# Layer 0's modulation by blocks: from split float32r passes with the activations stationary to plain float32 products with the raw weight block stationary

## The chip, the core and the metric

The kernel runs on one core of a Trainium2 chip. Five engines work side by side, each on its own queue of instructions in order: PE (TensorE, matrix products), DVE (VectorE), ACT (ScalarE), POOL (GpSimd) and SP (SyncE, which here only issues loads). They wait for each other by semaphores. The metric is device time of one execution in microseconds (us).

## The reference, cut to what matters

Two layers of a diffusion backbone run over 512 latent tokens and 256 context tokens, 1024 features wide. Each layer draws its shifts, scales and gates from two conditioning vectors, one per stream:

```python
c_act, cc_act = silu(c), silu(c_ctx)                # [1024] each
mod_l = c_act  @ w_mod[l] + b_mod[l]                # w_mod[l]: [1024, 6144]
mod_c = cc_act @ w_mod[l] + b_mod[l]
sh1, sc1, g1, sh2, sc2, g2 = split(mod_l, 6)        # likewise for the context
h = rmsnorm(x, g_norm1) * (1 + sc1) + sh1           # feeds the mixer's input product w_in
x = x + g1 * mixer(h); x = x + g2 * mlp(rmsnorm(x, g_norm2) * (1 + sc2) + sh2)
```

The outputs `sc1`, `sh1` of layer 0 stand ahead of everything else; `g1` and `sh2` are needed only later.

## The kernel before, in words

All matrix products keep about float32 accuracy with float32r passes, which hold fewer bits: each operand is split in a high and a low part, and three passes (high by high, high by low, low by high) add up. Weights come in blocks of 128 x 1024 float32 (512 KB). The class `Weights` streams them in the order of their use: SP loads a block into one of four `raw` buffers, ACT casts it to the high part `whi` (L142), DVE subtracts to get the low part `wlo` (L143). A `raw` buffer is free again when both are done. Loads run three blocks ahead of use, splits two. The loads of `x` stand in the same SP queue (`load`), in program order.

The modulation of a layer has three groups of 2048 outputs: group 0 is `sh1`, `sc1`; group 1 is `g1`, `sh2`; group 2 is `sc2`, `g2`. Groups 0 and 1 of layer 0 go "by blocks" on PE: 8 pieces (`n`) of 512 outputs, each from 4 weight blocks (`kk`), 32 blocks in all. All other groups go by rows on DVE (`mod_rows`, tile `junk`) and are not touched. `mod_block` makes one block: for each of its two halves of 128 features, the activations `ct` (128 x 4: high and low part of both vectors) are the stationary operand, and 512 columns of `whi`, then of `wlo`, stream through: four matmuls of 512 columns into rows 0 to 3 of the PSUM tile `modps` (L369). After the fourth block ACT copies the 4 x 512 result to `row`, PE turns it with four transposes into `modt` (L376), and two small DVE additions (L381, L385) leave the outputs on partitions.

Where these blocks stand: `first_tiles` makes pieces 2 and 3 (the scales `sc1`) first, each followed by scaling half of the features (`s`, then `xh` on ACT and `xl` on DVE), and runs the first two tiles of the input product (`lx0`, `lx1`, PSUM `inps`) on half of the features at a time. Blocks of pieces 0 and 1 (the shifts) stand between the products of the second half. Then come `spread` (1/rms of the tokens on all partitions), `first_bias` (PSUM `bias`: the shifts' product, added to the finished tiles) and the steps of the table `ORDER`; its steps `f1`, `f2`, `f4` each make one, two or four of the 16 blocks of group 1, between the products of the tiles `pu0`, `pu1`, `kv0`, `kv1`, `kr` and of the recurrent gates (`gps`). `nsum` sums the squares of `x` over the features with plain float32 products of 128 x 128 stationary and one moving column. A second kind, `lsum`, `qs`, `kns`, does the same later on.

Within each engine a scheduler orders the instructions when the kernel is built.

Of the kernel before, what the change touches and what calls it, by code (L numbers as in the profile page):

```python
# [9 lines left out]
F32 = mybir.dt.float32  # L10
F32R = mybir.dt.float32r
# [3 lines left out]
ALU = mybir.AluOpType  # L15
# [3 lines left out]
L = 512  # L19
# [7 lines left out]
EPS = 1e-6  # L27
# [9 lines left out]
KD = D // 128  # L37
# [26 lines left out]
# The engine of each kind of step, in either layer: s(calar), v(ector) or g(psimd).  # L64
# [12 lines left out]
def by_rows(l, g, h):  # L77
    """Half h of a modulation group: by rows of the transposed weight (vector engine), or by blocks (tensor engine)."""
    return l > 0 or (g, h) in ((2,0),(2,1))
# [32 lines left out]
class Weights:  # L112
    """Streams the weight blocks in the order of their use and keeps each as two parts whose sum is exact."""
# [7 lines left out]
    def advance(self, at):  # L121
        K, nc = self.K, self.K.nc
        while self.loaded < min(len(self.order), at + 1 + self.loads):
            name = self.order[self.loaded]
            raw = K.rawp.tile([128, 1024], F32, tag="raw", name="raw")
            K.load(raw, K.wb[BLOCK_AT[name]])
            self.raw[name] = raw
            self.loaded += 1
        while self.split < min(len(self.order), at + 1 + self.splits):
            name = self.order[self.split]  # L130
            raw = self.raw.pop(name)
            hi = K.wp.tile([128, 1024], F32R, tag="w", name="whi")
            if name[2:] == ("kr",):
                # Twice the same 64 columns: the first take the low part, so that one pass carries both parts.
                nc.scalar.copy(hi, raw)
                r3, h3 = (t.rearrange("p (k m) -> p k m", k=KD)[:, :, 0:64] for t in (raw, hi))
                nc.vector.tensor_tensor(h3, r3, h3.bitcast(F32), ALU.subtract)
                self.parts[name] = (hi,)
                self.split += 1
                continue  # L140
            lo = K.wp.tile([128, 1024], F32R, tag="w", name="wlo")
            nc.scalar.copy(hi, raw)  # L142
            nc.vector.tensor_tensor(lo, raw, hi.bitcast(F32), ALU.subtract)  # L143
            self.parts[name] = (hi, lo)
            self.split += 1
# [31 lines left out]
class Kernel:  # L177
# [41 lines left out]
    def times(self, what, out, in_, scale):  # L219
        """in_ times a value per partition."""  # L220
        e = PLACE[what][self.layer]
        if e == "s":
            return self.nc.scalar.activation(out, in_, AF.Copy, scale=scale)
        if e == "g":
            return self.nc.gpsimd.tensor_scalar(out, in_, scale, 0.0, ALU.mult, ALU.add)  # L225
        return self.nc.vector.tensor_scalar(out, in_, scale, None, ALU.mult)

    def plus(self, what, out, in_, bias):
        """in_ plus a value per partition."""
        if PLACE[what][self.layer] == "s":  # L230
            return self.nc.scalar.activation(out, in_, AF.Identity, bias=bias)
        return self.nc.vector.tensor_scalar(out, in_, bias, None, ALU.add)

    def mm3(self, lhs, rhs, segs, first, last):
        """Product of two split operands: segs lists (psum, lhs columns, rhs columns)."""
# [8 lines left out]
    def split(self, name, src, n):  # L244
        """The two float32r parts of src[:, :n]."""
# [5 lines left out]
    def rsqrt(self, v, n, r=None, sign=1.0):  # L251
        """sign / sqrt(v) on a tiny tile, refined by one Newton step."""
# [10 lines left out]
    def rsqrt_dve(self, v, n, r=None, sign=1.0):  # L263
        """1 / sqrt(v) on a tiny tile: a first guess from the bits of v, then three Newton steps."""
# [15 lines left out]
    def load(self, out, in_):  # L280
        """A load that keeps its place in the order of the loads."""
# [4 lines left out]
    def stage(self, name, tables=None):  # L286
        """From here on, functions of another table set: queued behind those of the set before."""
# [27 lines left out]
    def consts(self):  # L315
# [14 lines left out]
        self.ct = cp.tile([128, 8, 4], F32R, name="ct")  # L330
# [3 lines left out]
        nc.vector.tensor_copy(self.ct[:, :, 0:2], c3)  # L334
        nc.vector.tensor_tensor(self.ct[:, :, 2:4], c3, self.ct[:, :, 0:2].bitcast(F32), ALU.subtract)

    def decay(self, l):
        """-8 softplus(-lam) and its negative, softplus by max(u, 0) + log1p(exp(-|u|))."""
# [22 lines left out]
    def mod_block(self, l, g, n, kk):  # L361
        nc = self.nc
        hi, lo = self.w.get((l, "mod", g, n, kk))
# [3 lines left out]
        for j in range(2):  # L367
            for i, w in enumerate((hi, lo)):
                nc.tensor.matmul(ps[0:4, :], lhsT=self.ct[:, kk * 2 + j, :], rhs=w[:, j * 512:(j + 1) * 512],  # L369
                                 start=(kk == 0 and j == 0 and i == 0), stop=(kk == 3 and j == 1 and i == 1))  # L370
        if kk == 3:
            row = self.slot("row")
            self.move("mod.c", row[0:4, 0:512], ps[0:4, :])
            pt = self.psB("modt")
            for j in range(4):
                nc.tensor.transpose(pt[:, j * 4:j * 4 + 4], row[0:4, j * 128:(j + 1) * 128], self.ident[0:4, 0:4])  # L376
            p4 = pt[:, 0:16].rearrange("p (j h v) -> p h v j", j=4, h=2)
            at = l * NPRM + PRM["bm"][0] + g * 16 + n * 4
            b = self.prm[:, at:at + 4].unsqueeze(1).to_broadcast([128, 2, 4])
            t = self.tiny(8).rearrange("p (v j) -> p v j", v=2)  # L380
            nc.vector.tensor_tensor(t, p4[:, 1], b, ALU.add)  # L381
# [3 lines left out]
            nc.vector.tensor_tensor(m, p4[:, 0], t, ALU.add)  # L385

    def mod_rows(self, todo):
        """Modulation by rows of the transposed weight, for halves (layer, group, half): loads run one item ahead."""
# [37 lines left out]
    def norm_scale(self, l, which):  # L426
        """g * (1 + scale) for both streams; the shift's place."""
# [11 lines left out]
    def square(self, k, x, n, pool=False):  # L439
        """Adds the squares of one tile to the running sum."""  # L440
# [17 lines left out]
    def scaled(self, k, x, s, sh, ctx):  # L458
        """x * s as two parts, with the shift as further columns."""
# [12 lines left out]
    def token_sums(self, sq, cols, ps, at, step, nt, first, last):  # L472
        """ps[:, at + tt * step + ...] += column sums of sq with the selector cols, tokens on partitions."""
# [15 lines left out]
    def spread(self, r, nt):  # L489
        """A value per token, on all partitions: two psum tiles (tokens 0..511 and 512..767)."""  # L490
# [22 lines left out]
    def gemm_mod(self, ps, w, xs, ctx, hook=None, ks=range(KD), shift=True):  # L513
        """Product with the modulated stream; psum columns as the stream's, or from 256 on without ctx."""
# [18 lines left out]
    def scaled_out(self, ps, ctx, name="t"):  # L533
        """psum times the tokens' 1/rms; the bias of either stream is in columns L and L + 1."""
# [46 lines left out]
    def lru_gates(self, l, i, xc, xcs, w):  # L581
        """Sigmoid and tanh parts of both directions."""
# [58 lines left out]
    def pool_mix(self, l, i, ps, ctx):  # L641
        """Window means minus the input, for the streams apart; each as two parts."""
# [58 lines left out]
    def lat_sums(self, zs, nt):  # L701
        """Sums of squares of a low-rank stream, tokens on partitions."""
# [19 lines left out]
    def query_eps(self, zs, nt):  # L722
        """The guard of the queries' norm, QK EPS, over the squared 1/rms of their low-rank stream, which the
        product with w_uq leaves out: it divides out of the norm everywhere else."""
# [4 lines left out]
    def query_lat(self, l, j, z, n):  # L729
        """z times its norm weight, as two parts."""  # L730
# [21 lines left out]
    def tables(self, l):  # L752
        """Rotation table times the norm weights, of the queries and of the keys' shared part."""
# [8 lines left out]
    def key_rope(self, z, tk):  # L762
        """The rotated shared key part, twice in rows 64..127 of two tiles, and its sums of squares per token;
        z holds the products with the weight's low part in rows 0..63, with its high part in rows 64..127."""
# [19 lines left out]
    def values(self, l, pp, half, kvn, w, vt):  # L784
        """Values with tokens on partitions: per pair of heads and half of the keys, [128, 3, (He Le Lo Ho) x 64]."""
# [16 lines left out]
    def key_part(self, l, p, kvn, w, kx):  # L802
        """Keys of a pair of heads, unrotated part: into rows 0..63 of the two tiles; squares."""
# [14 lines left out]
    def key_sums(self, l, p, sq, krv, early):  # L818
        """1/rms of the pair's keys, tokens on partitions."""
# [11 lines left out]
    def key_scale(self, l, p, r):  # L831
        """1/rms of the pair's keys, a row per head on all partitions."""
# [35 lines left out]
    def query_scale(self, sq, ctx, early):  # L868
        """-1 / (rms sqrt(QK)) of the head's queries, per token."""
# [33 lines left out]
    def transposed(self, ps2, keys):  # L903
        """Two query tiles' weights with keys on partitions: per half of the keys [128, 3, 256], as two parts."""
# [40 lines left out]
    def first_tiles(self):  # L945
        """The first products start on half of the features, and before the shift is there: its product is added
        to the finished tiles."""
# [74 lines left out]
    def mixer(self, l):  # L1022
        """The steps of a mixer, in the order of ORDER."""
# [145 lines left out]
        def project(h, m, ks):  # L1169
            """Adds the products of some of the parts to a tile of the output projection."""  # L1170
# [11 lines left out]
        def add_to(h, m, src):  # L1182
            """The tile of the residual stream with the gated product added."""
# [184 lines left out]
def _tables():  # L1368
    """Constants of the shapes: rotation factors, reciprocal window counts, selectors."""
# [34 lines left out]
def _rows(w, k):  # L1404
    """[K, M] -> [128, k tiles of M]: contraction rows on partitions."""
# [101 lines left out]
```

## Time and profile before

| | |
|---|---|
| median of 3 runs | 1653.0 us (1649.77 to 1654.8) |
| span of the profiled execution | 1650.7 us |
| PE | 96% of the span, 9519 matmul records |
| DVE, ACT, POOL | 68%, 41%, 22% |
| mean granted TensorE clock | 0.978 of 2.4 GHz |

Only the span of the profiled execution is listed; its last instruction ends with it. It lies 2.3 us under the median and within the range of the three runs. "Busy" of PE counts each matmul from its start to its modelled end, and these overlap: a busy PE can be a slow PE. The granted clock is the share of 2.4 GHz that PE got (1.00, or 0.50 at 1.2 GHz).

### The profile page before, as it was taken

The numbers are of one execution on the slowest core, as the hardware profiler recorded it, in microseconds if no ns is written. First come the engines' busy times: TensorE is split into PE (matmuls) and PEld (weight loads), VectorE is DVE, ScalarE is ACT, GpSimd is POOL, SyncE is SP. The second block draws the span as 40 slices with busy tenths as digits, with TensorE's granted clock in tenths as the row PEclk, the third lists the DMA queues.
The fourth block names the chain that finished last, engine by engine and source line by source line (L and its number), as shares of the span: only waits on it lengthen the run. The fifth ranks groups of instructions, "written<-read, shape, count | busy, mean of one in ns | idle before, by whom it ended". The sixth has DMA issues, their size and how long they took to land.

```text
span 1650.7 us, 24064 instructions
## 1 busy us (share of the span) xinstructions
PE 1582.8 (96%) x9519; PEld 1380.6 (84%) x9519; DVE 1122.0 (68%) x1810; ACT 680.4 (41%) x1078; POOL 368.2 (22%) x376
## 2 busy tenths in 40 slices
PE   5989999999999999999999999888999999999998
PEld 3668888889888888888888889787888989989897
DVE  8797888998767557837737646698987654545352
ACT  5557556646433123123213333745665432323131
POOL 4175434542300000000000232356454000000000
PEclk7999989999999999999999999999999999999999
DMA  6545211354234423524523430320334323323302
GB/s 251 198 150 185 81 58 37 94 185 152 82 97 144 142 89 119 187 78 128 166 90 120 142 109 21 121 71 20 97 122 141 103 90 96 97 90 93 100 27 102
DMA packets 54016, 184.57 MB, mean 112 GB/s; under 512 B 6624, under 2 KB 7264, under 8 KB 53904
## 3 DMA queue, kind: packets, MB, share of 16 engines
q1 hardware_dynamic: 49680, 166.49, 31.0%
q0 software_dynamic: 4224, 16.55, 2.8%
q8 instruction: 75, 1.23, 0.3%
q14 instruction: 37, 0.30, 0.1%
HBM read 170.90 MB, written 12.12 MB: 111 GB/s over the span
## 4 chain that ended last, share of the span: by engine, by line
PE 76%; DVE 15%; issue 4%; ACT 3%; POOL 1%; DMA 1%; SPq 0%; DVEq 0%; ACTq 0%; POOLq 0%
PE f L241 55%; PE wo L241 5%; PE inps L241 4%; PE sc L241 3%; DVE wlo L143 3%; PE tp L914 2%; DVE p L897 1%; PE modps L369 1%; DVE junk L413 1%; PE qp L241 1%; PE pv L936 1%; PE pv L937 1%; DVE ptl L922 1%; PE gps L241 1%; PE kns L823 1%
## 5 line engine op out<-in xcount | busy, mean ns | idle before, releaser
L142 ACT CAST whi<-raw 128x1024 fp32r<-128x1024 f32 x210 | 219.6, 1048 | 657.2 <-PE f L241 550.7
L143 DVE TENSOR_TENSOR wlo<-raw,whi 128x1024 fp32r<-128x1024 f32 x210 | 276.3, 1318 | 35.3 <-ACT whi L142 32.6
L241 PE MATMUL f<-xh,whi 128*128 128x258 f32 (+2 forms) x1024 | 234.6, 310 | 1.0 <-DVE tf L539 1.0
L241 PE MATMUL f<-xl,whi 128*128 128x258 f32 (+2 forms) x1024 | 234.5, 310 | 0.0
L241 PE MATMUL f<-xh,wlo 128*128 128x258 f32 (+2 forms) x1024 | 234.1, 310 | 0.0
L241 PE MATMUL f<-hh,wlo 128*128 128x512 f32 (+1 forms) x768 | 232.2, 356 | 0.0
L241 PE MATMUL f<-hl,whi 128*128 128x512 f32 (+1 forms) x768 | 231.9, 356 | 0.0
L241 PE MATMUL f<-hh,whi 128*128 128x512 f32 (+1 forms) x768 | 231.3, 356 | 0.0
L1276 DVE SCALAR_TENSOR_TENSOR xo<-f,mod,xo 128x512 f32<-128x512 f32 x96 | 60.5, 658 | 195.6 <-PE f L241 195.6
L413 DVE SCALAR_TENSOR_TENSOR junk<-modraw,cb 128x1024 bf16<-128x1024 f32 x128 | 161.8, 1275 | 21.9 <-DMA modraw<-in_wb_dram 21.5
L241 PEld LDWEIGHTS f<-xh,whi 128*128 128x128 f32 x1024 | 157.8, 189 | 12.5 <-PE f L241 1.2
L241 PEld LDWEIGHTS f<-xl,whi 128*128 128x128 f32 x1024 | 158.2, 189 | 11.4
L241 PEld LDWEIGHTS f<-xh,wlo 128*128 128x128 f32 x1024 | 157.9, 189 | 11.3
L539 DVE TENSOR_TENSOR tf<-f,rb 128x770 f32<-128x770 f32 (+1 forms) x64 | 52.8, 826 | 159.1 <-PE f L241 150.2
L241 PEld LDWEIGHTS f<-hh,whi 128*128 128x128 f32 x768 | 126.5, 188 | 22.4
L241 PEld LDWEIGHTS f<-hh,wlo 128*128 128x128 f32 x768 | 126.3, 188 | 22.5
L241 PEld LDWEIGHTS f<-hl,whi 128*128 128x128 f32 x768 | 126.4, 188 | 22.3
L463 POOL CAST xh<-mod 128x2 fp32r<-128x2 f32 x24 | 10.6, 441 | 466.8 <-PE f L241 466.8
L225 POOL TENSOR_SCALAR p<-p,sm 128x768 f32<-128x768 f32 (+1 forms) x80 | 70.4, 880 | 117.3 <-DVE sm L899 81.1
L241 PE MATMUL inps<-xh,whi 128*128 128x512 f32 (+1 forms) x352 | 87.3, 331 | 7.3 <-ACT xh L467 5.6
L305 ACT ACTIVATE p<-p,sm 128x768 f32<-128x768 f32 (+1 forms) x80 | 68.2, 853 | 57.4 <-DVE p L897 56.8
L241 PE MATMUL inps<-xl,whi 128*128 128x512 f32 (+1 forms) x352 | 86.4, 326 | 3.1 <-DVE xl L468 3.1
(290 smaller groups left out, 2909.9 us busy)
## 6 DMA issues: line engine op xcount, KB each, us to landing
raw<-in_wb_dram SPq DMA_DIRECT2D x212, 512.0 KB, 3.6
modraw<-in_wb_dram SPq DMA_DIRECT2D x64, 512.0 KB, 3.5
kb<-kd POOLq DMA_DIRECT2D x16, 384.0 KB, 4.3
x<-in_x_dram SPq DMA_DIRECT2D x8, 384.0 KB, 7.0
xo<-in_x_dram SPq DMA_DIRECT2D x8, 384.0 KB, 3.4
xp<-xo POOLq DMA_DIRECT2D x8, 384.0 KB, 3.5
xo<-xp SPq DMA_DIRECT2D x8, 384.0 KB, 3.1
xd<-xo POOLq DMA_DIRECT2D x8, 256.0 KB, 2.4
```

The costliest lines, as they stand in the source:

```text
L142: nc.scalar.copy(hi, raw)
L143: nc.vector.tensor_tensor(lo, raw, hi.bitcast(F32), ALU.subtract)
L225: return self.nc.gpsimd.tensor_scalar(out, in_, scale, 0.0, ALU.mult, ALU.add)
L241: nc.tensor.matmul(ps, lhsT=a[:, ca], rhs=b[:, cb], start=first and i == 0, stop=last and i == 2)
L305: ins = self.nc.scalar.activation(out, in_, func, **kw)
L369: nc.tensor.matmul(ps[0:4, :], lhsT=self.ct[:, kk * 2 + j, :], rhs=w[:, j * 512:(j + 1) * 512], start=(kk == 0 and j == 0 and i == 0), sto ...
L413: nc.vector.scalar_tensor_tensor(junk, r, 1.0, c, ALU.mult, ALU.mult, accum_out=acc[l, g][:, v * 16 + i:v * 16 + i + 1])
L539: nc.vector.tensor_tensor(t[:, 0:n], ps[:, o:o + n], self.rb[:, 0:n], ALU.mult)
L823: nc.tensor.matmul(ps[:, tt:tt + 7:6], lhsT=sq[:, tt * 128:(tt + 1) * 128], rhs=self.cst[:, CST_SELK:CST_SELK + 2], start=True, stop=True)
L897: nc.vector.tensor_scalar(p[:, 0:keys], s, rq[:, qt:qt + 1], None, ALU.mult, ALU.min, accum_out=nb)
L914: nc.tensor.transpose(ps[:, j * 256 + q * 128:j * 256 + (q + 1) * 128], ps2[q][:, kt * 128:(kt + 1) * 128], self.ident)
L1276: nc.vector.scalar_tensor_tensor(x[:, a:a + e], ps[:, a:a + e], mod[:, v, 8 + m:9 + m], x[:, a:a + e], ALU.mult, ALU.add)
```

## The change

A block of layer 0's modulation is no longer split: its `raw` tile goes to PE as it is. `mod_block` makes eight plain float32 matmuls per block. In each, a 128 x 128 piece of the raw weight is stationary and two columns of the activations `cs` (one per conditioning vector) move. Pieces of 128 outputs land on partitions straight away, in 8 columns of `modps`, so the copy to `row`, the transposes and one of the two DVE additions go. The `raw` buffer of a modulation block is free only when PE has read it. `ct` and its two small DVE instructions go. Nearly all other lines of the difference are comments and docstrings that are taken out, which moves line numbers (a helper at L241 stands at L245 now, L369 at L373).

```diff
@@ class Weights, advance
             raw = self.raw.pop(name)
+            if name[1] == "mod":
+                self.parts[name] = (raw,)
+                self.split += 1
+                continue
             hi = K.wp.tile([128, 1024], F32R, tag="w", name="whi")
@@ consts
-        self.ct = cp.tile([128, 8, 4], F32R, name="ct")
+        self.cs2 = cs
...
-        nc.vector.tensor_copy(self.ct[:, :, 0:2], c3)
-        nc.vector.tensor_tensor(self.ct[:, :, 2:4], c3, self.ct[:, :, 0:2].bitcast(F32), ALU.subtract)
@@ mod_block
-        hi, lo = self.w.get((l, "mod", g, n, kk))
+        w = self.w.get((l, "mod", g, n, kk))[0]
...
-        for j in range(2):
-            for i, w in enumerate((hi, lo)):
-                nc.tensor.matmul(ps[0:4, :], lhsT=self.ct[:, kk * 2 + j, :], rhs=w[:, j * 512:(j + 1) * 512],
-                                 start=(kk == 0 and j == 0 and i == 0), stop=(kk == 3 and j == 1 and i == 1))
+        for i in range(4):
+            for j in range(2):
+                k = kk * 2 + j
+                nc.tensor.matmul(ps[:, i * 2:i * 2 + 2], lhsT=w[:, j * 512 + i * 128:j * 512 + (i + 1) * 128],
+                                 rhs=self.cs2[:, k * 2:k * 2 + 2], start=k == 0 and i == 0, stop=k == KD - 1 and i == 3, skip_group_check=True)
         if kk == 3:
-            row = self.slot("row")
-            self.move("mod.c", row[0:4, 0:512], ps[0:4, :])
-            pt = self.psB("modt")
-            for j in range(4):
-                nc.tensor.transpose(pt[:, j * 4:j * 4 + 4], row[0:4, j * 128:(j + 1) * 128], self.ident[0:4, 0:4])
...
-            nc.vector.tensor_tensor(t, p4[:, 1], b, ALU.add)
...
-            nc.vector.tensor_tensor(m, p4[:, 0], t, ALU.add)
+            nc.vector.tensor_tensor(m, ps[:, 0:8].rearrange("p (j v) -> p v j", v=2), b, ALU.add)
```

How the change moves instructions is seen at three places. The first is DVE's queue ahead of the first scales `s`. (`dk` are the 52 tiny steps of the decay constants, `mod` the outputs.) Before:

```order
L381 TENSOR_TENSOR ty<-modt,prm 128x8
L977 COPY ct<-cst 16x128
L353 TENSOR_SCALAR dk_7_586<-dk_7_586 128x4
L353 TENSOR_SCALAR dk_7_625<-dk_7_625 128x4
L385 TENSOR_TENSOR mod_0_183<-modt,ty 128x2x4
L352 TENSOR_TENSOR dk_7_586<-dk_7_586,dk_6_585 128x4
L352 TENSOR_TENSOR dk_7_625<-dk_7_625,dk_6_624 128x4
L965 SCALAR_TENSOR_TENSOR s_113<-mod_0_183,prm 128x2x4
```

and now, where `raw` and `whi` are those of the tiles `lx0` and `lx1`:

```order
L359 TENSOR_SCALAR dk_11_543<-dk_10_542 128x4
L359 TENSOR_SCALAR dk_11_582<-dk_10_581 128x4
L360 TENSOR_SCALAR dk_10_542<-dk_10_542 128x4
L360 TENSOR_SCALAR dk_10_581<-dk_10_581 128x4
L147 TENSOR_TENSOR wlo<-raw,whi 128x1024 x2
L381 TENSOR_TENSOR mod_0_171<-modps,prm 128x2x4
L961 SCALAR_TENSOR_TENSOR s_102<-mod_0_171,prm 128x2x4
L464 SCALAR_TENSOR_TENSOR xl<-x,s_102,xh 128x512
```

The scales stood in the midst of the `dk` steps; now they stand behind all of them and behind the two subtractions for `lx0` and `lx1`.

The second place is PE's queue in the second half of the first two tiles, where the shifts' blocks stand between products. Before:

```order
L369 MATMUL modps<-wlo,ct 4x512
L369 MATMUL modps<-whi,ct 4x512
L369 MATMUL modps<-wlo,ct 4x512
L369 MATMUL modps<-whi,ct 4x512
L369 MATMUL modps<-wlo,ct 4x512
L241 MATMUL inps<-xl,whi 128x256
L241 MATMUL inps<-xh,wlo 128x512
L241 MATMUL inps<-xh,wlo 128x256
```

and now, in a pattern that repeats six times:

```order
L245 MATMUL inps<-xh,whi 128x512
L245 MATMUL inps<-xh,whi 128x256
L245 MATMUL inps<-xl,whi 128x512
L245 MATMUL inps<-xl,whi 128x256
L245 MATMUL inps<-xh,wlo 128x512
L245 MATMUL inps<-xh,wlo 128x256
L373 MATMUL modps<-cs,raw 128x2 x8
```

Six products of the tile and the eight short products of a whole modulation block take turns.

The third place is PE's queue at the recurrent gates. Before:

```order
L369 MATMUL modps<-whi,ct 4x512
L369 MATMUL modps<-wlo,ct 4x512
L369 MATMUL modps<-whi,ct 4x512
L369 MATMUL modps<-wlo,ct 4x512
L369 MATMUL modps<-whi,ct 4x512
L241 MATMUL gps<-xch,whi 128x512
L241 MATMUL gps<-xch,whi 128x256
L241 MATMUL gps<-xcl,whi 128x512
```

and now:

```order
L373 MATMUL modps<-cs,raw 128x2 x16
L245 MATMUL gps<-xch,whi 128x512
L245 MATMUL gps<-xch,whi 128x256
L245 MATMUL gps<-xcl,whi 128x512
L245 MATMUL gps<-xcl,whi 128x256
L245 MATMUL gps<-xch,wlo 128x512
L245 MATMUL gps<-xch,wlo 128x256
L373 MATMUL modps<-cs,raw 128x2 x14
```

Around each six products of a gate stand now 12 to 16 short ones of one or two modulation blocks. SP's queue issues the same loads in the same order; from the start of the attention on, the order of all engines is that of before but for some exchanged neighbours in its first part.

## Rows read from the trace of the kernel before

**Rows 1.** The page: the span, and the granted clock in 40 slices.

```profile
span 1650.7 us, 24064 instructions
...
PEclk7999989999999999999999999999999999999999
```

**Rows 2.** Window: busy us (count) of PE, PEld, DVE, ACT, POOL; PEclk, DMA, GB/s.

```profile
0.00:40.00 40.00, 21.23 (x78) 12.21 (x79) 33.13 (x78) 21.22 (x29) 18.29 (x17) 0.79 0.65 247
```

**Rows 3.** Groups of instructions, 0 to 170 us: busy, mean ns, idle before.

```profile
L143 DVE TENSOR_TENSOR wlo<-raw,whi 128x1024 fp32r<-128x1024 f32 x44 | 62.5, 1433 | 13.4 <-ACT whi L142 13.4
L142 ACT CAST whi<-raw 128x1024 fp32r<-128x1024 f32 x45 | 46.4, 1041 | 19.0 <-PE modps L369 9.9 <-DMA raw<-in_wb_dram 5.4 <-PE inps L241 3.5
...
L369 PE MATMUL modps<-wlo,ct 128*4 128x512 f32 x64 | 28.8, 451 | 7.6 <-DVE wlo L143 7.6
L369 PE MATMUL modps<-whi,ct 128*4 128x512 f32 x64 | 28.7, 448 | 6.0 <-ACT whi L142 6.0
...
L376 PE MATMUL modt<-cst,row 4*128 4x4 f32 x32 | 3.6, 215 | 3.0 <-ACT row L216 3.0
```

**Rows 4.** The chain that ended last, 30 to 144 us: start, us, what.

```profile
30.33 4.51 DMA x<-in_x_dram
...
45.09 2.06 PE nsum L478 x12
47.15 4.71 PE modps L369 x11
...
57.99 2.88 PE modps L369 x12
...
66.64 0.80 PE spread L498 x6
...
69.29 1.92 PE bias L1008 x32
...
96.04 1.94 PE gps L241 x6
...
120.77 8.45 PE inps L241 x48
...
136.50 1.04 PE gps L241 x6
...
138.25 5.63 PE inps L528 x32
```

**Rows 5.** Timeline of PE at two places: start, us, what, records.

```profile
45.94 1.21 PE L478 MATMUL nsum<-ones,acc 128*128 128x1 f32 x5
47.01 0.59 PE L369 MATMUL modps<-wlo,ct 128*4 128x512 f32 x1
...
209.07 1.39 PE L478 MATMUL lsum<-ones,lsq 128*128 128x1 f32 x12
...
211.66 0.37 PE L241 MATMUL vps<-whi,lath 128*128 128x256 f32 x1
```

**Rows 6.** Windows of half a us: columns as in rows 2.

```profile
213.00:213.50 0.50, 0.50 (x5) 0.50 (x5) 0.44 (x1) 0.50 (x2) 0.50 (x1) 0.55 0.00 0
216.50:217.00 0.50, 0.19 (x1) 0.19 (x2) 0.48 (x2) 0.00 (x1) 0.50 (x2) 1.00 0.66 188
```

**Rows 7.** Timeline of ACT, POOL and DVE, 4 to 22 us.

```profile
4.87 1.04 ACT L142 CAST whi<-raw 128x1024 fp32r<-128x1024 f32 x1 [0.91 <-DMA raw<-in_wb_dram]
...
12.09 5.29 POOL L445 TENSOR_TENSOR sq<-x 128x768 f32<-128x768 f32 x3
...
16.01 1.39 DVE L349 TENSOR_TENSOR dk<-dk 128x4 f32<-128x4 f32 x1
...
19.20 0.16 DVE L352 TENSOR_TENSOR dk<-dk,dk 128x4 f32<-128x4 f32 x1
...
21.98 0.15 DVE L965 SCALAR_TENSOR_TENSOR s<-mod,prm 128x8 f32<-128x8 f32 x1
```

**Rows 8.** A window behind the modulation: columns as in rows 2.

```profile
172.00:176.00 4.00, 2.68 (x5) 1.51 (x5) 4.00 (x6) 0.57 (x2) 1.26 (x1) 0.51 0.46 131
```

More of the change, by code (lines that the diff above doesn't have):

```diff
@@ L366, in mod_block @@
         ps = self.modps
-        for j in range(2):
-            for i, w in enumerate((hi, lo)):
-                nc.tensor.matmul(ps[0:4, :], lhsT=self.ct[:, kk * 2 + j, :], rhs=w[:, j * 512:(j + 1) * 512],
-                                 start=(kk == 0 and j == 0 and i == 0), stop=(kk == 3 and j == 1 and i == 1))
-        if kk == 3:
-            row = self.slot("row")
-            self.move("mod.c", row[0:4, 0:512], ps[0:4, :])
-            pt = self.psB("modt")
-            for j in range(4):
-                nc.tensor.transpose(pt[:, j * 4:j * 4 + 4], row[0:4, j * 128:(j + 1) * 128], self.ident[0:4, 0:4])
-            p4 = pt[:, 0:16].rearrange("p (j h v) -> p h v j", j=4, h=2)
+        for i in range(4):
[3 more added lines that the diff above has]
+                                 rhs=self.cs2[:, k * 2:k * 2 + 2], start=k == 0 and i == 0, stop=k == KD - 1 and i == 3, skip_group_check=True)
+        if kk == 3:
             at = l * NPRM + PRM["bm"][0] + g * 16 + n * 4
             b = self.prm[:, at:at + 4].unsqueeze(1).to_broadcast([128, 2, 4])
-            t = self.tiny(8).rearrange("p (v j) -> p v j", v=2)
-            nc.vector.tensor_tensor(t, p4[:, 1], b, ALU.add)
             if (l, g) not in self.mod:
```

## The prediction

> **What bounds the kernel now.** I read the page first: the span and the slices of the clock [rows 1]. From the third slice to the last PE runs at nine tenths of full clock or more; only the start is slow. The change lies wholly within the first 150 us, and a window over the first 40 comes next [rows 2]: PE is busy 21.2 us of them and DVE 33.1, so the start waits for splits, loads and scales. The chain shows a second regime behind it [rows 4]: from `nsum` at 45.1 us to the product of `kr` at 138.25 most of it is PE, one group on the next. What lengthens PE's queue there moves the end; what relieves DVE counts only where PE waits for it. PE waited for parts of modulation blocks 7.6 + 6.0 us, and for `row` 3.0 [rows 3].
>
> **What goes.** 32 casts on ACT at 1.04 us (33 us) and 32 subtractions on DVE at 1.43 us as measured there (46 us) [rows 3]. Both are off PE, so they are worth at most PE's 13.6 + 3.0 us of waits. On PE 128 passes of 512 columns go: 0.24 us each at full clock (12 in 2.88 us) and 0.43 at half (11 in 4.71) [rows 4], together 30.7 or 54.8 us; and 32 transposes with 3.6 us busy, which overlap, so some 3 us [rows 3].
>
> **What comes.** 32 x 8 = 256 plain float32 products with a 128 x 128 stationary and two moving columns. Rows show the same shape with one column: `lsum`, `qs`, `nsum`. The 12 products of `lsum` and `qs` are 24 records (a plain float32 product is two, each with its own weight load) and take 211.66 - 209.07 = 2.59 us, so 0.108 us a record [rows 5]; at half clock five records take 47.01 - 45.94 = 1.07 us, 0.214 a record. A product costs 0.216 or 0.428 us, a block 1.73 or 3.42 us, against 0.96 or 1.71 before. All 256: 55.3 us at full clock, 109.6 at half. At full clock throughout PE gains 55.3 - 30.7 - 3 = 21.6 us of work; 16.6 us of waits go against it.
>
> **The clock is the larger term.** At 209.07 us, at full clock, PE began those 24 plain records. It had no idle time, and at 213.0 to 213.5 the granted clock fell to half (1.2 GHz), 4.0 us after they began, when products that stream 256 columns had already run for 1.4 us; it was back at 1.00 in the window from 216.5, some 4.8 us after streaming resumed [rows 5, 6].  So plain products of one or two columns do not hold the clock, though they fill PE's time. I take from these rows: it falls 4 us into a stretch ruled by such products, and rises 5 us into one ruled by streaming. Streaming products slow by 0.43/0.24 = 1.78 at half clock, plain ones by 1.98. In the new order six products of a tile (1.05 us at full) alternate with eight plain ones (1.73 us), so plain work rules [rows 4].
>
> A rule of the Trainium skill speaks otherwise (TensorE: Matmul & The Clock Gate, Part 1): the default state is throttled, activity releases it, and a PE that is kept busy without gaps stays warm. By it the sum would be that of the first rival; the row at 213 us disagrees, since PE had no gap there.
>
> **The walk along PE's queue**, by landmarks of the chain [rows 4].
>
> First scales. The blocks of piece 2 start when the first raw block has landed, at 4.87 us (where ACT began its cast before) [rows 7], at half clock: 32 x 0.428 = 13.7, so `modps` ends at 19.0 and the first block of piece 3 at 22.5. But `s` stands behind 52 `dk` steps and two subtractions on DVE. While POOL squares (three in 5.29 us from 12.09), a `dk` step of DVE waits for the POOL instruction under way: 1.39 us at 16.01, against 0.16 at 19.20, when POOL stands [rows 7]. In the new order POOL has four squares and three sums there in one go; at 1.6 us each (an estimate from the 5.29 us) they last from 10.5 to some 22 us and let through about one step each. The last 32 or so steps, which overlap to some 0.1 us apiece, take 3 us more. With the two subtractions I get 28.5 us for `s`, against 22.0; if POOL lets more through, 22. The first `xh` follows at about 29.3.
>
> First half of the tiles: 48 products of a tile are 8.45 us at full, 15.0 at half. Six plain ones stand among the first (2.6). With the rise 5 us into the streaming: 29.3 + 2.6 + 5 + 5.6 = 42.5 us.
>
> Then 26 plain products (4 us at full, 7.5 left at half: 7.2 us): `nsum` starts at 49.7, against 45.1. The loads of `x` that `nsum` needs stand in SP's queue behind one that waits for the buffer of `lx1`, so for its subtraction. They began at 30.3 before, 14.8 us ahead of `nsum` [rows 4]; now near 29, so the sums are there by 44. `nsum` at half: 2.6, to 52.3.
>
> Second half: 48 products and 56 plain ones in turn, at half clock throughout: 15.0 + 24.0 = 39.0, to 91.3; `spread` started at 66.6 before. `spread` 1.4, 16 plain 6.9: `bias` at 99.5, against 69.3: **30 us late**.
>
> `bias` 1.9, `pu0` 8.45, eight plain 1.7, `pu1` 8.45, with 2.2 us for the late rise: 22.8, so the gates start at 122.3, against 96.0. (Four of these 30 us come back: before, PE waited there for the convolution on DVE and for a split. That DVE work is done in time now.)
>
> Gates, first part: 24 products 4.2 and 54 plain 11.7 are 15.9 at full; 4 us at full and 11.9 x 1.9 at half: 26.6, to 148.9. `kv0`, pool, eleven plain, `kv1`: 8.45 + 2.2 + 1.0 + 2.4 + 8.45 = 22.5, to 171.4. Second part: 39 plain 8.4 and 24 products 4.2 are 12.6; 4 and 8.6 x 1.9: 20.3, to 191.7. `kr` started at 138.25: **53 us late**; its own rise adds 2.2.
>
> Behind it nothing changes but the phase. From 172 to 176 us PE stood 1.3 us and had half clock nearly throughout [rows 8]; DVE, which it waited for, has a head start now, so I give back 3 us. Sum: 1650.7 + 53.4 + 2.2 - 3 = 1703 us of span. The median stands 2.3 us above the span of before: **1705 us**.
>
> Edits at nothing: the `ct` steps and one small addition per piece on DVE, behind which nothing waits for long; the `raw` buffers that PE now frees. SP issues in order, so a held buffer delays the loads queued behind it, but at the 247 GB/s of the first window [rows 2] a block of 512 KB comes in 2.1 us, and PE works 3 to 5 us per block with the products between; where that cover fails a block costs 1 to 2 us, three or four times at most (5 us, in the range).
>
> **Rivals.** *The clock stays full* (0.07). PE has no idle time in the new stretches, but the row at 213 us is against it. Then: 29.3, first half to 41.3, plain and `nsum` 48.2, second half 68.7, `bias` 73, gates near 95, `kr` at 144 against 138.25: +6, about 1659 us.
>
> *Half the stretches stay full* (0.13): either the second half of the first tiles (39 shrinks to 20.5, with `spread` and its 16 products 22 us less) or both gate stretches (10.7 + 7.7 = 18 us less). For it: the rows hold only one long run of plain products at full clock, and none in which they alternate with streaming ones. Then 1683 to 1687 us.
>
> *Faster* (0.04). Relief of DVE reaches the path: `s` comes at 19.5, as soon as `modps` ends, not at 28.5. That is 9 us on the path, and 3 more of waits at the convolution; it decides only if the clock stays full from there, since the stretches cost 6 us then and 50 else. Price: 1659 - 12 = 1647 us. Against it stands the order of DVE, with the scales behind all `dk`.
>
> *No change* (0.02): the late stretches wait for something that I put on PE, and 50 us vanish in idle time that the rows do not show.
>
> **How the numbers follow.** The walk has 0.74. Its own range: `s` at 22 instead of 28.5 (-6), rises 2 us sooner at four places (-5), DVE's head start worth 8 instead of 3 (-5), against loads (+5), falls after 2 us instead of 4 (three times, +2 each) and nothing given back (+3): 1689 to 1719, widened upward for stretches whose waits I put at nothing: 1724. With the half-full case below it the range is 1678 to 1724; outside it are the rival of the full clock, faster, no change, and a tail of 0.06. Within 0.3% (5 us; less can't be told from no change with this measurement) lie no change and the edge of the full clock: 0.03. Faster 0.04, slower 0.93.
>
> **What would show it.** The windows of the changed kernel at 0.50 granted clock from the plain products ahead of `nsum` to `bias`, with PE busy all the time; `bias` near 100 us; half clock again at both gate stretches; `modps` records 0.21 us apart there; `kr` near 190 us. If `modps` records are 0.11 us apart and the clock is 1.00 in these stretches, the clock step is wrong and the result is near 1660. If `s` comes well ahead of 28 us, the step on DVE is wrong. It would also be wrong if a two-column product were costlier than a one-column one, or if PE waits for raw blocks.

## The result and the profile after

The changed kernel takes 1700.4 us (median of 4 runs, 1693.9 to 1709.4) against 1651.4 for the kernel before, measured beside it (4 runs, 1649.4 to 1654.8). The ratio is 1.0294, with a 95% interval of 1.0259 to 1.0330: 49 us slower, where 1705 (1678 to 1724) was forecast, 52 above the 1653.0 that the forecast started from. The profiled execution is the slowest of the four, so the time lost is read below from places in the program, and not from its span. One run of all those below, the fourth of `e11`, took 1.9% longer than the fastest of its kernel, and medians and ratios leave it out.

The page of the changed kernel, to be read against [rows 1]:

```profile
span 1707.6 us, 24623 instructions
...
PE 1652.9 (97%) x9871; PEld 1476.1 (86%) x9871; DVE 1079.4 (63%) x1768; ACT 646.3 (38%) x1038; POOL 355.2 (21%) x376
...
PEclk9577799899999999999999999998999999999999
```

The second slice of the clock, 43 to 85 us, fell from 9 to 5. (The first slice, 9 against 7, is no gain: the profile lists 1.00 there, but 16 records of `modps` take 3.54 us from 5.07 on, 0.221 us each, near the 0.214 of half clock in [rows 5].) Three windows show where (columns as in rows 2):

```profile
40.00:70.00 30.00, 30.00 (x164) 28.49 (x162) 6.36 (x16) 4.57 (x10) 0.00 (x0) 0.66 0.40 123
70.00:100.00 30.00, 30.00 (x147) 28.94 (x148) 6.06 (x10) 4.36 (x6) 2.21 (x21) 0.50 0.45 161
100.00:140.00 40.00, 40.00 (x225) 36.84 (x224) 21.50 (x27) 13.33 (x18) 14.03 (x18) 0.80 0.32 103
```

PE has work in every one of these 100 us, and DVE and ACT, which were to be relieved, stand nearly idle (DVE 12.4 of 60 us). Yet PE's granted clock is 0.66, then 0.50, half speed for 30 us on end. The chain of the changed kernel passes through the same stages as [rows 4] and is nothing but PE from 28.92 us on:

```profile
5.07 3.54 PE modps L373 x16
...
41.81 6.64 PE modps L373 x52
48.45 2.56 PE nsum L474 x12
...
60.61 2.13 PE inps L245 x6
62.74 3.21 PE modps L373 x16
...
87.28 1.38 PE spread L494 x6
88.66 6.62 PE modps L373 x32
95.28 3.43 PE bias L1004 x32
...
108.70 1.68 PE modps L373 x16
110.38 8.54 PE inps L245 x48
118.93 1.06 PE gps L245 x6
...
132.16 4.91 PE modps L373 x24
...
158.24 10.11 PE inps L245 x48
...
188.43 7.93 PE inps L524 x32
```

Sixteen records of `modps` (one block) take 3.21 us at 62.74 and 1.68 at 108.70; six products of a tile take 2.13 at 60.61, against 1.06 in [rows 4] (48 in 8.45). In the gates 24 records take 4.91 us, 0.205 each. Half-us windows show the granted clock change between such stretches:

```profile
46.00:46.50 0.50, 0.50 (x6) 0.50 (x5) 0.14 (x1) 0.33 (x1) 0.00 (x0) 0.86 0.85 279
46.50:47.00 0.50, 0.50 (x4) 0.50 (x4) 0.07 (x1) 0.50 (x2) 0.00 (x0) 0.50 0.97 352
...
59.50:60.00 0.50, 0.50 (x6) 0.50 (x7) 0.00 (x0) 0.00 (x0) 0.00 (x0) 1.00 0.89 369
60.00:60.50 0.50, 0.50 (x5) 0.50 (x4) 0.00 (x0) 0.00 (x0) 0.00 (x0) 0.51 0.96 393
...
100.50:101.00 0.50, 0.50 (x4) 0.41 (x3) 0.00 (x0) 0.00 (x0) 0.00 (x0) 0.53 0.45 180
101.00:101.50 0.50, 0.50 (x5) 0.46 (x4) 0.00 (x0) 0.00 (x0) 0.00 (x0) 1.00 0.06 25
```

It fell at 46.4, in the run of 52 plain records that began at 41.81, was back from 56.6 to 60.0, fell again in products that took turns with plain ones, and came back only at 101.0, in the run of `inps` products behind `bias`. PE was busy throughout. A rule of the Trainium skill (TensorE: Matmul & The Clock Gate, Part 1) says that a PE kept busy without gaps stays at full clock. These rows disagree, with busy as the profile counts it: PE at 30.00 of 30.00 us and a clock of 0.50.

### The profile page after: what moved, and what is told of

Read it like the earlier page. It is cut to its first block, busy times and chain, and to the rows that moved or that the text cites. A ratio compares the mean times of both kernels' runs of the same rounds, so it can differ in the third digit from the quotient of the medians.

```text
span 1707.6 us, 24623 instructions
## 1 busy us (share of the span) xinstructions
PE 1652.9 (97%) x9871; PEld 1476.1 (86%) x9871; DVE 1079.4 (63%) x1768; ACT 646.3 (38%) x1038; POOL 355.2 (21%) x376
## 4 chain that ended last, share of the span: by engine, by line
PE 81%; DVE 12%; issue 3%; ACT 2%; POOL 1%; DMA 1%; SPq 0%; DVEq 0%; POOLq 0%; ACTq 0%
PE f L245 53%; PE inps L245 7%; PE wo L245 5%; PE modps L373 4%; PE sc L245 3%; PE tp L910 2%; DVE wlo L147 1%; DVE p L893 1%; PE gps L245 1%; PE qp L245 1%; PE pv L932 1%; PE pv L933 1%; DVE junk L409 1%; DVE keh L221 1%; DVE rn L280 1%
## 5 line engine op out<-in xcount | busy, mean ns | idle before, releaser
L146 ACT CAST whi<-raw 128x1024 fp32r<-128x1024 f32 x178 | 186.6, 1049 | 691.8 <-PE f L245 551.5
L147 DVE TENSOR_TENSOR wlo<-raw,whi 128x1024 fp32r<-128x1024 f32 x178 | 227.3, 1278 | 56.1 <-ACT whi L146 50.1
L245 PE MATMUL f<-xh,whi 128*128 128x258 f32 (+2 forms) x1024 | 235.1, 311 | 1.0 <-DVE tf L535 1.0
L245 PE MATMUL f<-xh,wlo 128*128 128x258 f32 (+2 forms) x1024 | 234.4, 310 | 0.0
L245 PE MATMUL f<-xl,whi 128*128 128x258 f32 (+2 forms) x1024 | 234.4, 310 | 0.0
L245 PE MATMUL f<-hl,whi 128*128 128x512 f32 (+1 forms) x768 | 232.3, 357 | 0.0
L245 PE MATMUL f<-hh,wlo 128*128 128x512 f32 (+1 forms) x768 | 232.1, 356 | 0.0
L245 PE MATMUL f<-hh,whi 128*128 128x512 f32 (+1 forms) x768 | 232.0, 357 | 0.0
L245 PEld LDWEIGHTS f<-xh,whi 128*128 128x128 f32 x1024 | 158.1, 189 | 12.9 <-PE f L245 1.2
L245 PEld LDWEIGHTS f<-xl,whi 128*128 128x128 f32 x1024 | 158.0, 189 | 11.1
L245 PEld LDWEIGHTS f<-xh,wlo 128*128 128x128 f32 x1024 | 157.6, 189 | 11.3
L245 PEld LDWEIGHTS f<-hl,whi 128*128 128x128 f32 x768 | 126.6, 188 | 22.5
L245 PEld LDWEIGHTS f<-hh,wlo 128*128 128x128 f32 x768 | 126.5, 188 | 22.6
L245 PEld LDWEIGHTS f<-hh,whi 128*128 128x128 f32 x768 | 126.5, 188 | 22.1
L373 PEld LDWEIGHTS modps<-cs,raw 128*128 128x128 f32 x512 | 93.8, 283 | 7.8 <-issue 5.0
L245 PE MATMUL inps<-xh,whi 128*128 128x512 f32 (+1 forms) x352 | 93.1, 346 | 7.6 <-ACT xh L463 4.8
L373 PE MATMUL modps<-cs,raw 128*128 128x2 f32 x512 | 91.8, 312 | 5.5 <-DMA raw<-in_wb_dram 5.4
```

The costliest lines, as they stand in the source:

```text
L245: nc.tensor.matmul(ps, lhsT=a[:, ca], rhs=b[:, cb], start=first and i == 0, stop=last and i == 2)
L373: nc.tensor.matmul(ps[:, i * 2:i * 2 + 2], lhsT=w[:, j * 512 + i * 128:j * 512 + (i + 1) * 128], rhs=self.cs2[:, k * 2:k * 2 + 2], start=k ...
```

## The experiments

Three theories stood against each other. *Clock*: the plain products add some PE work, but most of the loss is that PE runs at half clock wherever products with two moving columns are frequent. *Work*: the plain products just occupy PE for longer (21.6 us by the prediction's sum), and the clock is a side effect. *Loads or weight loads*: raw buffers held by PE delay the loads, or the 512 loads of a 128 x 128 stationary keep PE slow. Ratios are to the kernel before, timed beside each.

**One half of the change at a time.** `e1` has the plain form for group 0 alone, `e2` for group 1 alone; the other half keeps the split passes of before.

```diff
+def plain(g, n):
+    return g == 0
...
-            if name[1] == "mod":
+            if name[1] == "mod" and plain(*name[2:4]):
...
```

In `e2` the condition is `g == 1`.

> Only group 0 (shifts and scales, 16 blocks) goes as plain products; group 1 goes by split passes as before. Clock theory (plain products with two moving columns fill PE but do not hold the clock, and the half-clock stretches are the larger term): the half clock runs from the plain products ahead of nsum to bias as in the changed kernel, bias stands near 95 us, and the gates are back at full clock; kr at about 160 us, +22 to +26 us on before: 1673 to 1677 us. Work theory (only the longer occupation of PE by the plain records counts, the clock is incidental): half of the 21.6 us of extra work less the waits saved, at most +11: 1662 us or less. Load theory (raw buffers held by PE delay the loads): PE would show idle time ahead of modps.

> The converse: only group 1 (gates' blocks between pu0, kv0 and the recurrent gates) goes as plain products; group 0 by split passes as before. Clock theory: bias stays near 69 us, and half clock appears in both stretches of the recurrent gates, kr at 160 to 166 us, +22 to +28 us: 1673 to 1680 us. Work theory: at most +11: 1662 us or less, with the clock at 1.00 in the gates or without effect. If the two halves add up to the whole, the two effects are independent.

`e1`: 1678.7 us, ratio 1.0161 (1.0138 to 1.0184). `e2`: 1681.8 us, 1.0182 (1.0156 to 1.0208). The chain of `e1`:

```profile
87.10 1.38 PE spread L529 x6
...
91.89 2.45 PE bias L1039 x32
...
161.35 5.65 PE inps L559 x32
```

And that of `e2`:

```profile
69.11 3.43 PE bias L1039 x32
...
92.65 1.05 PE gps L249 x6
...
113.53 4.91 PE modps L408 x24
...
161.24 5.74 PE inps L559 x32
```

In `e1` `bias` comes 22.6 us late and `kr` (the last row) 23.1: all is lost ahead of `bias`, and the gates cost what they did. In `e2` `bias` is on time to 0.2 us and `kr` 23.0 us late. `e2`'s gates run 24 plain records in 4.91 us, 0.205 each: half clock. The work theory gave either of them at most 11 us; both times lie just under 2 us above the ranges of the clock theory. PE was busy for all of 40 to 100 us in `e1`, so its loads cost nothing there. The halves by time, 25.9 and 29.0 us, add up to 54.9 against 49.0 for the whole, which the intervals, 4 to 6 us either way, do not tell apart; by `kr` they add up to 46.1 against 50.2. Where the 4 us between the halves and the whole lie was not followed.

**The same products turned round.** `e3` keeps plain float32 and raw weights, and lets 512 columns of the raw block move past the two activation columns.

```diff
-        for i in range(4):
-            for j in range(2):
...
+        for j in range(2):
+            k = kk * 2 + j
+            nc.tensor.matmul(ps[0:2, :], lhsT=self.cs2[:, k * 2:k * 2 + 2], rhs=w[:, j * 512:(j + 1) * 512],
+                             start=k == 0, stop=k == KD - 1)
...
```

> All 32 blocks stay plain float32 with raw weights and no split, but the roles are exchanged: the two activation columns are stationary and 512 columns of the raw block move; two products per block half become two per block, 64 in all, with the row copy and four transposes per piece back. Clock theory (few moving columns are at fault, not float32): the granted clock stays at 1.00 in the stretches that were at 0.50; no row shows the price of a plain product of 512 columns, by bounds 0.48 us (two records of 0.24) to 0.96 us each, 31 to 61 us of PE for 64 products: 1640 to 1682 us. If plain float32 itself cannot hold the clock: half clock in the same stretches, 1690 us or more. Load theory: raw buffers are still held by PE, so the time stays near 1700 us.

1663.3 us, ratio 1.0067 (1.0046 to 1.0087). From the chain of `e3`:

```profile
54.50 1.81 PE modps L372 x4
...
62.43 3.46 DMA raw<-in_wb_dram
```

Windows of `e3`:

```profile
40.00:70.00 30.00, 27.97 (x107) 12.11 (x106) 7.49 (x19) 7.28 (x15) 1.43 (x12) 0.97 0.50 161
70.00:100.00 30.00, 30.00 (x163) 20.25 (x162) 19.68 (x25) 12.77 (x19) 11.59 (x24) 0.97 0.34 124
100.00:140.00 40.00, 39.75 (x167) 21.81 (x165) 18.25 (x21) 10.20 (x15) 20.97 (x22) 1.00 0.53 185
```

Four records in 1.81 us are 0.905 us a product, the upper bound of what was expected, and 64 of them 57.9 us. In the changed kernel 512 records would take 53.8 us at full clock (1.68 / 16 each). So `e3` gives PE more work than the changed kernel and is 37 us faster: its clock stays at 0.97 to 1.00. It isn't float32 alone that costs the clock. But the stationary operand is another here too, so `e3` doesn't tell the few moving columns from the weight loads. The load theory has a small share at most: PE stood 2.0 us between 40 and 70 us, where the chain passes through the load of a raw block (62.43).

**As much work without the form.** `e9` is the kernel before with 96 more streaming passes.

```diff
-                nc.tensor.matmul(ps[0:4, :], lhsT=self.ct[:, kk * 2 + j, :], rhs=w[:, j * 512:(j + 1) * 512],
+                for again in range(1 + (i == 1) + (i == 1 and j == 1)):
+                    nc.tensor.matmul(ps[0:4, :], lhsT=self.ct[:, kk * 2 + j, :], rhs=w[:, j * 512:(j + 1) * 512],
...
```

> The kernel before, with three more passes of wlo by ct in each of the 32 blocks (the low part's product is added two or three times, so the modulation is off in its last bits): 96 more streaming passes of 0.24 us, 23.0 us of PE at full clock, as much as the plain products add to PE's work (21.6 us). Clock theory: PE's granted clock stays as before; what lies in PE's waits is hidden, so +8 to +18 us: 1661 to 1671 us. Work theory: a like amount of PE work costs a like time, so about as slow as the changed kernel, 1690 us or more.

1668.4 us, ratio 1.0083 (1.0070 to 1.0096): 14 to 15 us for 23 us of added work, as the clock theory had it. Its clock is 1.00 where the changed kernel's is 0.66 and 0.50:

```profile
40.00:70.00 30.00, 29.08 (x153) 17.61 (x152) 19.01 (x28) 14.79 (x23) 4.05 (x2) 1.00 0.47 155
70.00:100.00 30.00, 27.11 (x171) 20.68 (x169) 23.39 (x32) 17.46 (x24) 12.91 (x35) 1.00 0.31 105
```

**The same products with more moving columns.** `e12` and `e11` are the changed kernel with each activation column read 64 or 16 times over: 128 or 32 moving columns, the same 256 products, stationaries and places. `C` is 128 or 32.

```diff
-                                 rhs=self.cs2[:, k * 2:k * 2 + 2], start=k == 0 and i == 0, stop=k == KD - 1 and i == 3, skip_group_check=True)
+                wide = self.cs2[:, k * 2:k * 2 + 2].unsqueeze(2).to_broadcast([128, 2, C // 2])
+                nc.tensor.matmul(ps[:, i * C:(i + 1) * C], lhsT=w[:, j * 512 + i * 128:j * 512 + (i + 1) * 128],
+                                 rhs=wide, start=k == 0 and i == 0, stop=k == KD - 1 and i == 3, skip_group_check=True)
...
```

> The changed kernel with the same 256 plain float32 products and the same 128 x 128 pieces of raw weight stationary in the same places, but 128 moving columns in each: either vector's column is read 64 times over, and one column of each 64 results is used. Few-columns theory: what lost the clock is the moving columns, not float32 and not the weight loads; so the clock stands at 1.00 from nsum to bias and in the gates. A record costs at least the 0.107 us of two columns, and by the 0.45 us of 512 columns in the kernel with the roles exchanged some 0.11; 512 records take 55 to 60 us, and the time is 1655 to 1668 us though no product got shorter. Weight-load theory (512 loads of a 128 x 128 stationary, one per record, keep PE from full clock): half clock in the same stretches, 1690 us or more.

> The same with 32 moving columns (either column read 16 times over). Few-columns theory gives no number between two and 128 columns: if it behaves as two columns, half clock and about 1700 us; if it behaves as 128, full clock and about 1660 us; a part of the stretches at half clock would give 1670 to 1690. Records at 0.107 us apart at full clock and 0.214 at half in any case. Weight-load theory: as two columns, 1690 us or more.

`e12`: 1658.4 us, ratio 1.0032 (1.0017 to 1.0048). `e11`: 1679.8 us, 1.0161 (1.0144 to 1.0178). Windows of `e12`:

```profile
40.00:70.00 30.00, 30.00 (x244) 28.96 (x243) 6.78 (x19) 4.99 (x11) 2.49 (x9) 1.00 0.57 178
70.00:100.00 30.00, 30.00 (x222) 27.40 (x221) 24.13 (x29) 12.84 (x20) 14.49 (x30) 1.00 0.45 152
100.00:140.00 40.00, 39.95 (x286) 37.00 (x285) 14.59 (x19) 11.51 (x16) 19.27 (x21) 1.00 0.62 202
```

The same windows of `e11`:

```profile
40.00:70.00 30.00, 30.00 (x201) 28.64 (x200) 6.27 (x16) 4.57 (x10) 0.00 (x0) 0.83 0.47 144
70.00:100.00 30.00, 30.00 (x223) 27.44 (x222) 20.10 (x28) 12.17 (x18) 12.04 (x33) 1.00 0.50 168
100.00:140.00 40.00, 40.00 (x206) 37.70 (x204) 12.28 (x17) 9.12 (x12) 20.77 (x25) 0.66 0.41 133
```

This is the plainest test. No product got shorter (in the chain of `e12` 16 records take 1.79 us, against 1.68 in the changed kernel at full clock), none went, and the kernel is 42 us faster, with the clock at 1.00 in all three windows. The weight loads are the same 512, so they are not the cause. With 32 columns the clock fell ahead of `nsum`, at 45.2 us, stood at 1.00 again from 55.5 on while blocks and products of a tile took turns, and fell once more in the gates, at 103.3: a time in between. The chain of `e12` gives the price of the clock by stages:

```profile
46.38 1.24 PE nsum L478 x12
...
64.03 1.79 PE modps L376 x16
...
68.64 0.66 PE spread L498 x6
...
93.93 1.05 PE gps L245 x6
```

From the end of `nsum` to `spread` it needs 21.0 us, where the changed kernel needs 36.3 (51.01 to 87.28). `kr` begins at 143.6 in `e12`'s timeline, so the gates take 49.7 us against 69.5 (118.93 to 188.43). These two stages give 35 of the 45 us that lie between the two kernels at `kr`.

**The same work in another order.** In `e4` the seven blocks that alternate with the second half of the first tiles stand behind it.

```diff
-                self.mod_block(0, 0, i, k - 4)
+        for i in range(2):
+            for kk in range(4):
+                self.mod_block(0, 0, i, kk)
```

> As the changed kernel, but the seven shift blocks that alternate with the products of the second half of the first two tiles all stand behind these products: 48 streaming products in one run, then 56 plain ones. The work is the same. Clock theory: the clock rises some 5 us into the run of 48 and they end at full clock; spread starts 4 to 8 us earlier than the 87.28 us of the changed kernel, about 1693 us. Work theory and load theory: spread at the same time, no change from 1700 us.

1693.5 us, ratio 1.0247 (1.0225 to 1.0269). The chain of `e4`:

```profile
50.57 10.80 PE inps L245 x48
61.37 19.77 PE modps L373 x112
81.14 1.38 PE spread L494 x6
```

The 48 products together take 10.80 us, where 15.0 was my sum for half clock throughout, and `spread` starts 6.1 us earlier with the same instructions. The interval of the ratio just overlaps that of the changed kernel, so this reading rests on the landmarks more than on the time. A long run of plain records still loses the clock: in windows of 1 us it is 1.00 from 56 to 65 us and 0.50 from 66 on.

**The late scales.** `e5` puts the `dk` steps behind the first scales on DVE's queue, `e7` does the same to the kernel before.

```diff
-        nc.vector.tensor_scalar(t[0], lam, -1.0, None, ALU.mult)
+        ins = nc.vector.tensor_scalar(t[0], lam, -1.0, None, ALU.mult)
+        if self.w.order is not None:
+            self.tc.add_manual_dep(ins.ins, self.scales.name, mybir.DependencyInfo(
+                mybir.DependencyClass.NoSync, mybir.DependencyReason.DATA), reason="behind the scales")
...
```

> The changed kernel, with the dk steps of the decay constants put behind the first scales s in the order of DVE's queue. Collision theory (dk steps each wait for POOL's squares and hold up s): s at 19.5 to 21 us instead of 26.4, the first inps at 21 to 22.5 instead of 27.3, nsum and spread 5 to 7 us earlier than 48.5 and 87.3; about 1694 us. Rival (s waits for the raw load and the two subtractions ahead of it anyway): s at 25 us or later, no change.

> The kernel before with the dk steps behind the first scales s in DVE's queue, nothing else. If dk steps were on the path to the first scales there: s at 18 to 20 us instead of 22.0, and 0 to 3 us off the time (1650 to 1653). If the products of the start wait for something else (xl and the subtractions on DVE, loads): no change.

In the changed kernel's timeline of DVE two `dk` steps mostly take 1.5 to 1.9 us as long as POOL squares and sums, and 0.28 afterwards:

```profile
10.54 1.57 DVE L354 TENSOR_TENSOR dk<-dk,dk 128x4 f32<-128x4 f32 x2
...
20.11 1.86 DVE L355 TENSOR_SCALAR dk<-dk 128x4 f32<-128x4 f32 x2
21.89 0.28 DVE L354 TENSOR_TENSOR dk<-dk,dk 128x4 f32<-128x4 f32 x2
```

POOL in the same stretch:

```profile
12.10 4.30 POOL L441 TENSOR_TENSOR sq<-x 128x768 f32<-128x768 f32 x3
16.37 5.58 POOL L452 TENSOR_TENSOR acc<-acc,sq 128x768 f32<-128x768 f32 x3
```

In `e5` `s` starts at 20.05 instead of 26.4, still behind the two subtractions, `nsum` at 42.80 and `spread` at 81.60, both 5.7 us earlier, as expected. The time is 1698.8 us, ratio 1.0272 (1.0259 to 1.0286), where about 1694 us was expected: its interval lies within that of the changed kernel, so the gain is seen in the profile and not shown by the time. `e7`: `s` at 15.5 instead of 22.0, `nsum` only 0.6 us earlier (44.5), 1652.5 us, ratio 0.9985 (0.9974 to 0.9997): too little to call a change. In the kernel before, the start waits for other things than the scales.

**A better version?** `e10` takes the turned form of `e3` for the scales alone, `e13` the 128 columns for group 0, `e14` for group 0 and the first piece of group 1, all three with the `dk` steps behind. Their edits are those shown, with another condition in `plain` (`g == 0 and n >= 2`, `g == 0`, `(g, n) <= (1, 0)`).

> Only the 8 blocks of the scales (pieces 2 and 3 of group 0) go as plain float32 products, with the two activation columns stationary and 512 columns of the raw block moving; the other 24 blocks are split as before, and the dk steps stand behind the first scales. Clock theory: streaming plain products hold the clock, and the scales come where PE waits for DVE's splits, so s at 16 to 18 us instead of 22.0, nsum at 39 to 42 us instead of 45.1, and 3 to 6 us off: 1646 to 1650 us. Rival (the gain is lost again to a later wait, for the loads of x or the convolution on DVE): bias at 69 us as before, 1652 to 1654 us.

> A version put together from the runs: group 0 (16 blocks) as plain products with 128 moving columns, group 1 split as before, and the dk steps behind the first scales. By the pieces measured: nsum at 41 us (46.2 in the kernel with 128 columns, less the 5.5 us that the dk steps cost), bias at 67.5, then as before 26.8 us to the gates and 48.7 to lsum, which starts at 143 us against 144.8: about 1651 us, no change that can be told from before. Rival (the loads of x, queued behind the raw buffers, hold nsum back to 44 us or later): bias at 70 us, 1653 to 1655 us.

> As the version with group 0 in 128 columns, with the first piece of group 1 (4 blocks, those between pu0, pu1 and the first gate) in that form too. With all blocks plain and 128 columns the way from bias to the gates took 21.1 us against 26.8, since DVE's convolution had no subtractions in its queue, and the gates' own stretch took 7.6 us more. If the first can be had without the second: gates at 89 us against 96.0, lsum at 138 against 144.8, about 1646 us. Rival (the subtractions for the second piece stand among the convolution anyway): no gain on the version with group 0 alone, about 1651.

`e10`: 1655.8 us, ratio 1.0007 (0.9996 to 1.0018); `s` at 15.6 us, but `nsum` at 46.2 and `bias` at 70.6: the early scales gained nothing, as the rival had it, though the time lies above the rival's range too. What holds `nsum` there was not tested. `e13`: 1651.1 us, 0.9986 (0.9972 to 1.0000), `nsum` at 42.4 and `lsum` at 142.2, nearly as expected. `e14`: 1649.7 us, 0.9988 (0.9976 to 1.0001), the first gate at 90.1 where 89 was expected, `lsum` at 144.3 where 138 was. None differs from before by more than a measurement can tell. The expectation of `e14` rested on a misreading of mine, which is told in the next section.

## Why the prediction was right, point by point

The likeliest case came true, by its own mechanism. The landmarks of the walk against the chain of the changed kernel:

| start of | predicted, us | measured, us | before, us |
|---|---|---|---|
| `s` | 28.5 | 26.4 | 22.0 |
| `nsum` | 49.7 | 48.45 | 45.09 |
| `spread` | 91.3 | 87.28 | 66.64 |
| `bias` | 99.5 | 95.28 | 69.29 |
| gates | 122.3 | 118.93 | see below |
| `kr` | 191.7 | 188.43 | 138.25 |

- **Price of a record**: 0.105 us at full clock and 0.201 at half, where `lsum` and `nsum` gave 0.108 and 0.214. A second moving column cost nothing that shows.
- **Scales**: the `dk` steps ahead of `s` were the cause (`e5`), slowed while POOL worked. `s` was over-priced by 2.1 us: POOL worked from 10.6 to 21.9 us, as summed, but two steps went through with each of its seven instructions, where about one was assumed. The parts of the sum were loose besides: 5.29 us for three squares are 1.76 apiece, not 1.6, and 22 + 3 us with two subtractions of 1.43 make 27.9, not 28.5.
- **Second half at half clock**: nearly. The clock stood at 1.00 from 56.6 to 60.0 us, in the first products of that stage; 39 us were summed, 36.3 measured. With the scales it is what put `kr` 3.3 us ahead of the forecast.
- **Gates at half clock**: 69.4 us summed, 69.5 measured, and 49.7 with 128 columns. That the sum fits to 0.1 us is luck: the first part took 25.2 us for 26.6, the second 20.1 for 20.3, and between them `kv0` to `kv1` took 24.2 for 22.5, since the 22 plain records ahead of `kv1` brought half clock there too (10.11 us for its 48 products, from 158.24), which was not summed. In the second part the blocks stand 23, 8, 1 and 7 products at a time, and not 12 to 16 as in the first.
- **Raw buffers**: PE's idle time ahead of `modps` is 5.5 us in all, 5.1 of it before the first block has landed at the start, so later loads cost 0.4 us, where up to 5 were allowed for.
- **`kr` 53 us late**: 50.2. Its own rise: 2.3 us, as summed (7.93 against 5.63).
- **Given back, 3 us**: the first product of the MLP (`f`) starts at 492.9 us against 443.2, so 49.7 of the 52.5 us are left, close to the 49.0 between the medians. That DVE's head start gave them back is not shown. The profiled execution lost 5.9 us more by the first `f` of the second layer (1338.9 against 1283.3), where both kernels hold the same work; the other three runs were 7.7 to 15.5 us shorter, and what caused it stays open.

One step was misread, without harm to the sum. I took the gates to begin at 96.0 us before, and so found four of thirty us given back there. But 96.04 in [rows 4] is the second group of gate products, the first that the chain happens to hold. The timeline of the kernel before shows the first, and the wait between them:

```profile
89.35 0.51 PE L241 MATMUL gps<-xch,whi 128*128 128x512 f32 x2
...
94.60 0.59 PE L369 MATMUL modps<-wlo,ct 128*4 128x512 f32 x1 [3.81 <-DVE wlo L143]
```

From `bias` to the first gate the changed kernel lost another 3.4 us (23.6 against 20.2), by `bias` and the first products of `pu0` at half clock. The wait for `wlo` that it saves lies inside the gates' stage, which cost 48.9 us before. The sum walks forward to `kr` and has no term with the 96.0, so the error didn't reach it; in `e14`, whose gain was reckoned from it, it did.

Two readings of the kernel before were too smooth. In [rows 1] the clock is not at nine tenths from the third slice on: the sixth, from 206 us, is an 8. And of the 93 us of its chain from `nsum` to `kr`, 38 are not PE: between 80.2 and 119.7 us it runs mostly through DVE. PE itself stood 5.3 us between 89 and 120 us, so not all that lengthened its queue there had to move the end.

The rival of the full clock was priced at 1659 us, with `kr` at 144, and nothing changed but the clock. `e12`, which has that clock, takes 1658.4, with `kr` at 143.6.

## What to carry to other kernels

A product with few moving columns can be dear beyond its own time: where plain float32 products of two columns were frequent here, PE was busy without a gap and ran at half clock, and everything between them slowed too. (Other types with as few columns were not run.) When a matrix times a vector must go on PE, make the large operand the moving one, or, with the weight stationary, widen the moving operand: here 128 columns instead of two cost 0.007 us a record and gave 42 us back. Neither form beat the split passes of before (ratios 1.0067 and 1.0032 to it): by the prediction's sum 21.6 us of work on PE come at full clock, and only 16.6 us of PE's waits go. Price such a change by the granted clock of its stage, and check in the timeline that a landmark taken from the chain is the first of its kind.

## What the runs showed of the hardware

- Reading one activation column 64 times over as the moving operand needs no copy in memory and little time: 0.112 us a record with 128 columns against 0.105 with two.
- A plain float32 product with 512 moving columns takes 0.905 us at full clock, two records of 0.45, against 0.24 for a float32r pass of the same columns [rows 4].
- 32 moving columns gave a clock between that of two and that of 128: 0.83 from 40 to 70 us, 1.00 to 100 and 0.66 to 140, with PE busy in all of the three windows.
- Two of DVE's tiny steps (128 x 4) took 0.28 us with POOL idle and mostly 1.5 to 1.86 us while POOL squared and summed.
